# A two-layer hybrid trunk on one core: x and the per-channel parameters handed over by channel, layer 0's sums of squares by a matmul with ones

## The chip, the cores and the metric

One core of a Trainium2 chip runs the whole program. The metric is the device time of one execution in microseconds, as a median over runs. The kernel before took 1278.25 us (median of 3 runs, 1276.6 to 1279.12).

## The reference

Two layers run over 256 tokens of 2048 channels. Cut to what the change touches, each layer is:

```
h    = x * rsqrt(mean(x*x over channels) + eps) * pre_norm_w     # pre-norm, one factor per token
proj = h @ w_in                                                  # 2048 -> 9248 columns: u, gate, z, x, B, C, dt
A    = pool_mixer(u, pool_mix_w, pool_scale) * silu(gate)        # scale per channel
B    = ssd(silu(conv(x,B,C; conv_w, conv_b)), dt; dt_bias, a_log, d_skip), gated by z, times ssd_norm_w
x    = x + rms_norm(concat(A, B) @ w_out, post_norm_w)
```

## The kernel before, in words

**Layout.** Activations stand by channel: a tile `hs` holds, for each of 16 groups of 128 channels (k = 0 to 15), 256 tokens in two parts, a rounded high part and the rest (the low part), 512 columns in all. Weights are split in the same way. They stream in as units of 512 input rows by 512 output columns (`raw`, 1 MB, three buffers). Each unit is split in two halves, a and b, by ScalarE (`wh`, L141) and VectorE (`wl`, L142), five buffers each. A chunk is one 512-column block of the output: four units, u0 to u3 for the first chunk, u4 to u7 for the second. For each 128 by 128 block, TensorE does a wide matmul (high weights by 512 columns, L351) and a narrow one (low weights by the 256 high columns, L353). Here that is called a pair. A chunk has 64 pairs.

**The start of layer 0.** x comes by token in four pieces of 512 channels, into `t` tiles. TensorE turns them by 128 by 128 transposes against an identity (L305). ScalarE makes the high part from the turned block in PSUM, times the pre-norm weight (L314), and VectorE makes the low part (L315). `first_unit` writes out the order of u0 by hand, in single k: its wide and narrow matmuls are L620 and L626, its weight splits L156 and L162 (512 columns wide). Matmuls on the identity (L253) fill TensorE ahead of it. The pre-norm weight is loaded as 32 rows and turned too (L261, L263).

**Sums of squares.** ScalarE squares the untransposed pieces and sums along the row (L322), which gives one number per token. `token_rstd` and `rstd_diag` turn it into a diagonal matrix, and `rstd_spread` multiplies ones by it (L342), so that every partition has the row of factors, copied to `rb` (L344). The factor is applied late, on the output of the projection (L399 on GpSimd). The second chunk (column block C) starts with the 64-column dt block, eight matmuls L725 twice. `dt_chain` multiplies the dt block by `rb` (L422), and two transposes on TensorE follow (L431).

**Parameters.** `load_params` loads four tables as rows and three as broadcast rows. After twelve background steps it turns them by two transposes (L283, L284) and copies them (L285, L289, L290).

**Order.** A list scheduler sets the order of each engine by priorities; each engine then runs its queue strictly in that order. `behind(ins)` puts an instruction after another one of the same engine. Transfers go out from SP and from ScalarE (ACT) and use eight semaphores in turn, so a transfer is issued when the one eight places earlier has landed.

Of the kernel before, what the change touches and what calls it, by code (L numbers as in the profile page):

```python
# [8 lines left out]
F32 = mybir.dt.float32  # L9
# [32 lines left out]
def hybrid_kernel(ctx: ExitStack, tc, x, pre_norm_w, w_in, pool_mix_w, pool_scale, conv_w, conv_b,  # L42
                  dt_bias, a_log, d_skip, ssd_norm_w, w_out, post_norm_w, out):
# [73 lines left out]
    def emit_raw():  # L117
        i = stream["raw"]
        r = wts.tile([P, 4, CW], F32, name="raw", tag="raw", bufs=NRAW)
        src = units[i].rearrange("(k p) c -> p k c", p=P)  # L120
        if i < 2:
            for a, b in (((0, 1), (1, 2), (2, 3), (3, 4)), ((0, 2), (2, 4)))[i]:
                stream["dma"] = nc.sync.dma_start(out=r[:, a:b], in_=src[:, a:b])
        else:
            stream["dma"] = nc.sync.dma_start(out=r, in_=src)
        raws[i] = r
        stream["raw"] += 1
# [66 lines left out]
    def load_pieces(src, between=None):  # L194
        xp.clear()
        for c in range(4):
# [3 lines left out]
            if between is not None and c == 0:  # L200
                for a, b in ((0, 2), (2, 4)):
                    nc.scalar.dma_start(out=v[:, :, a * P:b * P], in_=piece_src[:, :, a * P:b * P])
            else:
                nc.sync.dma_start(out=v, in_=piece_src)
            xp.append(v)
            if between is not None and c < 3:
                between()
# [10 lines left out]
    ones = const.tile([P, P], F32, name="ones")  # L218
    nc.vector.memset(ones, 1.0)
# [29 lines left out]
    pre_cols = const.tile([P, DEPTH * NK], F32, name="pre_cols")  # L249
    def keep_busy(dst, n, after=None):  # L250
        with behind(after):
            for _ in range(n):
                ins = nc.tensor.matmul(dst[:, 0:P], ident, ident, start=True, stop=True, skip_group_check=True)  # L253
        return ins

    with tc.high_priority():
        idle = aux()
        filler = keep_busy(idle, 3)
        pp = aux()
        with behind(filler):  # L260
            pre_t = nc.tensor.transpose(out=pp[:, 0:DEPTH * NK], in_=pre_rows,  # L261
                                        identity=ident[0:DEPTH * NK, 0:DEPTH * NK])
        pre_copy = nc.vector.tensor_copy(pre_cols, pp[:, 0:DEPTH * NK])  # L263
        filler = keep_busy(idle, 4, pre_t)
# [3 lines left out]
    def load_params(l):  # L268
        rows = work.tile([56, P], F32, name="rows", tag="rows", bufs=1)
        nc.sync.dma_start(out=rows[0:16], in_=pool_scale[l].rearrange("(a p) -> a p", p=P))  # L270
        nc.sync.dma_start(out=rows[16:32], in_=ssd_norm_w[l].rearrange("(a p) -> a p", p=P))
        nc.sync.dma_start(out=rows[32:56], in_=conv_b[l].rearrange("(a p) -> a p", p=P))
        rows2 = work.tile([96, P], F32, name="rows2", tag="rows2", bufs=1)
        nc.sync.dma_start(out=rows2, in_=conv_w[l].rearrange("k (a p) -> (k a) p", p=P))
        hb = const.tile([P, 3, NH], F32, name=f"hb{l}")
        nc.sync.dma_start(out=hb[:, 0], in_=dt_bias[l].partition_broadcast(P))
        nc.sync.dma_start(out=hb[:, 1], in_=a_log[l].partition_broadcast(P))
        nc.sync.dma_start(out=hb[:, 2], in_=d_skip[l].partition_broadcast(P))
        for _ in range(12):
            yield  # L280
        cols = const.tile([P, 152], F32, name=f"cols{l}")
        pa = aux()
        nc.tensor.transpose(out=pa[:, 0:56], in_=rows, identity=ident[0:56, 0:56])  # L283
        nc.tensor.transpose(out=pa[:, 56:152], in_=rows2, identity=ident[0:96, 0:96])  # L284
        turned = nc.vector.tensor_copy(cols, pa[:, 0:152])  # L285
        dcol = const.tile([P, 16], F32, name=f"dcol{l}")
        dv = hb[:, 2].rearrange("p (j two) -> p two j", two=2)
        with behind(turned):
            nc.vector.tensor_copy(dcol[0:HD], dv[0:HD, 0])  # L289
            nc.vector.tensor_copy(dcol[HD:P], dv[HD:P, 1])  # L290
        prm[l] = {
            "scale": cols[:, 0:16], "norm": cols[:, 16:32], "convb": cols[:, 32:56],
            "convw": cols[:, 56:152].rearrange("p (k a) -> p k a", k=KCONV), "d": dcol,
            "dtb": hb[:, 0], "alog": hb[:, 1],
# [309 lines left out]
    def piece(c):  # L604
        pts = [None, None]
        transpose_piece(c, range(NT), pts)
        return split_piece(0, c, hs, pts)

    def first_unit(acc):

        pts = [None, None]

        def turn(ks, after):
            with behind(after):
                return transpose_piece(0, range(NT), pts, ks)

        def wide(kk, ms):
            wh = halves[kk // 2][0]
            for m in ms:
# [283 lines left out]
```

## Time and profile before

| | us |
|---|---|
| median of 3 runs | 1278.25 (1276.6 to 1279.12) |
| the profiled execution | 1279.39, its span 1277.7 |
| TensorE (PE) busy | 1265.1, 99% of the span |
| VectorE (DVE) busy | 916.4, 72% |
| ScalarE (ACT) busy | 707.8, 55% |
| GpSimd (POOL) busy | 198.5, 16% |
| DMA | 249.47 MB, mean 195 GB/s |

The span runs from the first to the last instruction; the time of an execution is 1.7 us longer. PE's matmuls overlap each other, so intervals between starts are read as the cost of one, not durations. Times in the rows below count from the start of the span.

### The profile page before, as it was taken

What the parts mean: (1) busy time and instruction counts of PE and PEld (TensorE: products, weight loads), DVE (VectorE), ACT (ScalarE), POOL (GpSimd) and SP (SyncE); (2) the same over time, 40 slices, a digit from 0 to 9 for tenths busy, and PEclk for the clock granted to TensorE, in tenths of its full rate; (3) what the DMA queues carried; (4) which work ended last, traced back from release to release, by engine and by line L of the source; (5) the groups of instructions that cost most, each with busy time, mean ns of one, the idle gap of its engine ahead of it and who ended that gap; (6) DMA issues with size and microseconds to landing.
All of it is one profiled execution on the core that took longest, in us unless ns stands there. A gap on an engine that the chain in (4) does not pass through costs nothing.

```text
span 1277.7 us, 17883 instructions
## 1 busy us (share of the span) xinstructions
PE 1265.1 (99%) x6978; PEld 1087.5 (85%) x6978; DVE 916.4 (72%) x1298; ACT 707.8 (55%) x894; POOL 198.5 (16%) x244
## 2 busy tenths in 40 slices
PE   9999999999999999999999999999999999999997
PEld 8888888888888888888878888888888888888886
DVE  5898778868778794444478978778788788844454
ACT  6656556566466574344374566566565565644442
POOL 0121312212213220000002122122113122200000
PEclk9999999999999999999999999999999999999999
DMA  8555455464474576555564645555654654855652
GB/s 277 200 199 199 165 200 205 152 235 166 164 246 150 212 269 209 189 188 189 188 212 164 220 168 175 204 192 169 226 198 144 219 201 162 296 198 197 197 188 77
DMA packets 127004, 249.47 MB, mean 195 GB/s; under 512 B 9304, under 2 KB 10152, under 8 KB 125640
## 3 DMA queue, kind: packets, MB, share of 16 engines
q1 hardware_dynamic: 124872, 237.27, 54.7%
q0 software_dynamic: 1504, 10.55, 2.2%
q8 instruction: 54, 0.88, 0.3%
q10 hardware_dynamic: 544, 0.52, 0.1%
q14 instruction: 30, 0.25, 0.1%
HBM read 244.06 MB, written 4.26 MB: 194 GB/s over the span
## 4 chain that ended last, share of the span: by engine, by line
PE 98%; ACT 1%; DVE 1%; issue 0%; DMA 0%
PE acc L351 43%; PE acc L353 22%; PE acc L788 9%; PE acc L790 9%; PE acc L789 9%; PE aux L543 1%; PE aux L548 1%; PE aux L725 1%; PE aux L305 1%; PE aux L509 1%; PE acc L620 0%; ACT t L322 0%; PE aux L568 0%; PE aux L497 0%; DVE t L806 0%
## 5 line engine op out<-in xcount | busy, mean ns | idle before, releaser
L351 PE MATMUL acc<-hs,wh 128*128 128x512 f32 x2288 | 804.7, 396 | 1.0 <-DVE hs L315 1.0
L142 DVE TENSOR_TENSOR wl<-raw,wh 128x1024 fp32r<-128x1024 f32 x430 | 531.9, 1246 | 251.8 <-ACT wh L141 251.3
L141 ACT ACTIVATE wh<-raw 128x1024 fp32r<-128x1024 f32 x430 | 450.4, 1058 | 411.3 <-PE acc L351 217.9
L353 PE MATMUL acc<-hs,wl 128*128 128x256 f32 x2288 | 638.7, 279 | 0.0
L351 PEld LDWEIGHTS acc<-hs,wh 128*128 128x128 f32 x2288 | 429.2, 188 | 98.9 <-DVE hs L315 1.5
L353 PEld LDWEIGHTS acc<-hs,wl 128*128 128x128 f32 x2288 | 431.5, 189 | 1.2 <-DVE wl L142 0.2
L399 POOL TENSOR_TENSOR t<-t,rb 128x256 f32<-128x256 f32 x144 | 142.1, 995 | 397.7 <-DVE t L393 369.0
L392 ACT COPY t<-acc 128x256 f32<-128x256 f32 x176 | 62.9, 366 | 70.2 <-PE acc L353 70.1
L788 PE MATMUL acc<-wh,pm 128*128 128x512 f32 x256 | 99.7, 390 | 0.0
L788 PE MATMUL acc<-wh,ms 128*128 128x512 f32 x256 | 99.7, 389 | 0.0
L790 PE MATMUL acc<-wh,ms 128*128 128x512 f32 x256 | 99.7, 389 | 0.0
L790 PE MATMUL acc<-wh,pm 128*128 128x512 f32 x256 | 99.7, 389 | 0.0
L789 PE MATMUL acc<-wl,ms 128*128 128x512 f32 x256 | 99.7, 389 | 0.0
L789 PE MATMUL acc<-wl,pm 128*128 128x512 f32 x256 | 99.6, 389 | 0.0
L393 DVE TENSOR_TENSOR t<-acc,t 128x256 f32<-128x256 f32 x176 | 71.4, 416 | 16.2 <-ACT t L392 15.3
L412 DVE SCALAR_TENSOR_TENSOR t<-t,cols,t 128x256 f32<-128x256 f32 x144 | 72.0, 529 | 0.1
L790 PEld LDWEIGHTS acc<-wh,ms 128*128 128x128 f32 x256 | 48.1, 188 | 10.1
L790 PEld LDWEIGHTS acc<-wh,pm 128*128 128x128 f32 x256 | 48.1, 188 | 10.0
L788 PEld LDWEIGHTS acc<-wh,ms 128*128 128x128 f32 x256 | 48.1, 188 | 10.0
L789 PEld LDWEIGHTS acc<-wl,pm 128*128 128x128 f32 x256 | 48.1, 188 | 9.9
L788 PEld LDWEIGHTS acc<-wh,pm 128*128 128x128 f32 x256 | 48.1, 188 | 9.9
L789 PEld LDWEIGHTS acc<-wl,ms 128*128 128x128 f32 x256 | 48.1, 188 | 9.8
(157 smaller groups left out, 848.3 us busy)
## 6 DMA issues: line engine op xcount, KB each, us to landing
raw<-in_w_in_dram SPq DMA_DIRECT2D x142, 1024.0 KB, 4.9
raw<-in_w_out_dram SPq DMA_DIRECT2D x64, 1024.0 KB, 5.1
t<-acs POOLq DMA_DIRECT2D x8, 1024.0 KB, 5.1
raw<-in_pool_mix_w_dram SPq DMA_DIRECT2D x8, 1024.0 KB, 5.2
t<-in_x_dram SPq DMA_DIRECT2D x7, 512.0 KB, 9.2
pwb<-in_post_norm_w_dram POOLq DMA_DIRECT2D x2, 1024.0 KB, 6.7
x_mid<-t SPq DMA_DIRECT2D x8, 256.0 KB, 2.7
t<-x_mid SPq DMA_DIRECT2D x4, 512.0 KB, 8.9
```

The source lines that it names most:

```text
L141: hi = nc.scalar.activation(out=wh, in_=r, func=AF.Copy)
L142: lo = nc.vector.tensor_tensor(out=wl, in0=r, in1=wh.bitcast(F32), op=ALU.subtract)
L305: ins = nc.tensor.transpose(out=pts[k4 % 2][:, o + T * P:o + (T + 1) * P], in_=xp[c][:, T, k4 * P:(k4 + 1) * P], identity=ident)
L351: nc.tensor.matmul(acc[m], wh[:, kk, cs], mov[:, k0 + kk, :], start=first and kk == 0, stop=False, skip_group_check=True)
L353: stream["mm"] = nc.tensor.matmul(acc[m][:, 0:SEQ], wl[:, kk, cs], mov[:, k0 + kk, 0:SEQ], start=False, stop=last and kk == 1, skip_group_ ...
L392: nc.scalar.copy(out=t[0:n], in_=acc[0:n, SEQ:CW])
L393: nc.vector.tensor_tensor(out=t[0:n], in0=acc[0:n, 0:SEQ], in1=t[0:n], op=ALU.add)
L399: nc.gpsimd.tensor_tensor(out=dest[:, m], in0=t, in1=rb, op=ALU.mult)
L412: nc.vector.scalar_tensor_tensor(out=dst[:, m], in0=pad[:, m, j:j + SEQ], scalar=cw[:, j, ct:ct + 1], in1=dst[:, m], op0=ALU.mult, op1=ALU ...
L788: nc.tensor.matmul(oacc[T], ah, wh[:, kk], start=first and kk == 0, stop=False)
L789: nc.tensor.matmul(oacc[T], ah, wl[:, kk], start=False, stop=False)
L790: nc.tensor.matmul(oacc[T], al, wh[:, kk], start=False, stop=last and kk == 1)
```

## The change

x is also handed over by channel (`x_by_channel`, 128 x 16 x 256: partition, k, token), the pre-norm weight as 128 x 32, and all other parameters of a layer as one table of 128 x 232, built by the host. In layer 0 x goes straight from the transfer into a tile `xt`, and L314 and L315 (now L291 and L292) read it there. Sums of squares are made over channels: four squares of 128 x 1024 (L303), three additions of that size and two smaller ones (L306, L308, L309), one matmul of ones by the total (L314), then square root (L316) and reciprocal (L317) on 128 x 256. The filler becomes eight matmuls on ones, and `load_params` is one transfer. Layer 1 keeps its transposes of x. x by token is still loaded for the residual.

```diff
-    pre_rows = const.tile([DEPTH * NK, P], F32, name="pre_rows")
-    nc.sync.dma_start(out=pre_rows, in_=pre_norm_w.rearrange("l (a p) -> (l a) p", p=P))
-    load_pieces(x_in, emit_raw)
+    nc.sync.dma_start(out=pre_cols, in_=pre_norm_by_channel)
+    xt = t16().rearrange("p a t c -> p (a t c)").rearrange("p (k s) -> p k s", s=SEQ)
+    def load_xt(a, b, queue=nc.sync):
+        queue.dma_start(out=xt[:, a:b], in_=x_by_channel[:, a:b])
+    load_xt(0, 1, nc.scalar)
+    load_xt(1, 2, nc.scalar)
+    emit_raw(lambda: load_xt(2, 4))
+    load_xt(4, 8)
+    emit_raw()
+    load_xt(8, 12)
+    load_xt(12, NK)
+    emit_raw()
...
+        for _ in range(8):
+            filler = nc.tensor.matmul(idle[:, 0:P], ones, ones, start=True, stop=True, skip_group_check=True)
...
-            src = pts[k4 % 2][:, (k4 // 2) * SEQ:(k4 // 2 + 1) * SEQ]
+            src = xt[:, k] if l == 0 else pts[k4 % 2][:, (k4 // 2) * SEQ:(k4 // 2 + 1) * SEQ]
...
+    def square_channels(c, total):
+        sq = t4()[:, :, 0:SEQ]
+        nc.scalar.activation(out=sq, in_=xt[:, 4 * c:4 * c + 4], func=AF.Square)
+        if c == 0:
+            return sq
+        nc.vector.tensor_tensor(out=total, in0=total, in1=sq, op=ALU.add)
+        if c == 3:
+            nc.vector.tensor_tensor(out=total[:, 0:2], in0=total[:, 0:2], in1=total[:, 2:4], op=ALU.add)
+            nc.vector.tensor_tensor(out=total[:, 0], in0=total[:, 0], in1=total[:, 1], op=ALU.add)
+        return total
+    def rstd_channels(total):
+        pb = aux()
+        nc.tensor.matmul(pb[:, 0:SEQ], ones, total[:, 0], start=True, stop=True)
+        rb = work.tile([P, SEQ], F32, name="rb", tag="rb", bufs=1)
+        nc.scalar.activation(out=rb, in_=pb[:, 0:SEQ], func=AF.Sqrt, scale=1.0 / D_MODEL, bias=eps)
+        nc.vector.reciprocal(out=rb, in_=rb)
+        return rb
...
+        hi, lo = filler, None
+        for kk in range(4):
+            with behind(hi, lo):
+                xs = split_piece(0, 0, hs, None, range(kk, kk + 1))
+            hi = first_hi(kk, xs[0])
+            lo = first_lo(kk, xs[1])
+            wide(kk)
+            if kk < 2:
+                narrow(kk)
...
-                    later["rb"] = rstd_spread(later["rd"])
+                    later["rb"] = rstd_spread(later["rd"]) if l else rstd_channels(later["sq"])
```

**PE at the start of the program.** `ident`, `ones` and `pre_rows` are inputs of fillers and transposes, `t_78` is the first piece of x, `hs`, `wh`, `wl` are the split activations and weights. Before:

```order
L253 MATMUL aux<-ident 128x128 x3
L261 MATMUL aux<-ident,pre_rows 128x32
L253 MATMUL aux<-ident 128x128 x4
L305 MATMUL aux<-ident,t_78 128x128 x2
L253 MATMUL aux<-ident 128x128
L620 MATMUL acc<-hs,wh 128x512 x2
L305 MATMUL aux<-ident,t_78 128x128 x2
```

and in the changed kernel:

```order
L261 MATMUL aux<-ones 128x128 x8
L609 MATMUL acc<-hs,wh 128x512 x4
L615 MATMUL acc<-hs,wl 128x256 x4
L609 MATMUL acc<-hs,wh 128x512 x4
L615 MATMUL acc<-hs,wl 128x256 x4
L609 MATMUL acc<-hs,wh 128x512 x8
L615 MATMUL acc<-hs,wl 128x256 x8
```

All 32 transposes of x are gone from the first chunk, and u0 runs in one piece.

**DVE in the first chunk, after u0.** `L315`/`L292` are the low parts of the activations, four k each; `L142`/`L145` are weight halves, in the order u1a, u1b, u2a and so on. Before:

```order
L142 TENSOR_TENSOR wl<-raw,wh 128x1024
L315 SCALAR_TENSOR_TENSOR hs<-aux,pre_cols,hs 128x256 x4
L142 TENSOR_TENSOR wl<-raw,wh 128x1024 x2
L315 SCALAR_TENSOR_TENSOR hs<-aux,pre_cols,hs 128x256 x4
L142 TENSOR_TENSOR wl<-raw,wh 128x1024 x2
L315 SCALAR_TENSOR_TENSOR hs<-aux,pre_cols,hs 128x256 x4
```

and in the changed kernel, where `t_222` is the running total and `t_283`, `t_336`, `t_359` are squares:

```order
L292 SCALAR_TENSOR_TENSOR hs<-s_78,pre_cols,hs 128x256 x4
L145 TENSOR_TENSOR wl<-raw,wh 128x1024 x2
L292 SCALAR_TENSOR_TENSOR hs<-s_78,pre_cols,hs 128x256 x4
L306 TENSOR_TENSOR t_222<-t_222,t_283 128x4x256
L292 SCALAR_TENSOR_TENSOR hs<-s_78,pre_cols,hs 128x256 x4
L306 TENSOR_TENSOR t_222<-t_222,t_336 128x4x256
L145 TENSOR_TENSOR wl<-raw,wh 128x1024 x2
L306 TENSOR_TENSOR t_222<-t_222,t_359 128x4x256
L145 TENSOR_TENSOR wl<-raw,wh 128x1024 x2
```

The first half of u2 stood ahead of the last eight low parts; now it stands behind all of them and behind two additions.

**DVE in the second chunk, up to the product of dt.** `L409`, `L412` (now `L405`, `L408`) are the convolution of block B, `L422` (now `L418`) is the product that the two transposes on PE wait for. Before:

```order
L409 TENSOR_SCALAR t_455<-t_527,cols_447 128x256 x2
L412 SCALAR_TENSOR_TENSOR t_455<-t_527,cols_447,t_455 128x256 x3
L142 TENSOR_TENSOR wl<-raw,wh 128x1024
L412 SCALAR_TENSOR_TENSOR t_455<-t_527,cols_447,t_455 128x256 x2
...
L412 SCALAR_TENSOR_TENSOR t_455<-t_527,cols_447,t_455 128x256 x6
L142 TENSOR_TENSOR wl<-raw,wh 128x1024 x2
L422 TENSOR_TENSOR t_616<-t_616,rb 64x256
```

and in the changed kernel:

```order
L317 RECIPROCAL rb<-rb 128x256
L405 TENSOR_SCALAR t_382<-t_455,cols_149 128x256 x2
L145 TENSOR_TENSOR wl<-raw,wh 128x1024
L408 SCALAR_TENSOR_TENSOR t_382<-t_455,cols_149,t_382 128x256 x2
...
L408 SCALAR_TENSOR_TENSOR t_382<-t_455,cols_149,t_382 128x256 x6
L145 TENSOR_TENSOR wl<-raw,wh 128x1024 x3
L418 TENSOR_TENSOR t_544<-t_544,rb 64x256
```

A reciprocal stands ahead of the convolution, and four weight halves instead of three stand between its start and the product of dt. On PE the two transposes that wait for it stand behind 85 and 86 matmuls of the chunk before, and behind 87 now. Behind this chunk the order on every engine is the same but for the parameter transposes and copies of layer 1.

## Rows read from the trace of the kernel before

**Rows 1.** The page: busy time of engines, and the chain that ended last, by engine.

```profile
PE 1265.1 (99%) x6978; PEld 1087.5 (85%) x6978; DVE 916.4 (72%) x1298; ACT 707.8 (55%) x894; POOL 198.5 (16%) x244
...
PE 98%; ACT 1%; DVE 1%; issue 0%; DMA 0%
```

**Rows 2.** Timeline of the start: start, duration, instruction, idle time before it.

```profile
5.48 0.63 ACT L156 ACTIVATE wh<-raw 128x512 fp32r<-128x512 f32 x1 [2.18 <-DMA raw<-in_w_in_dram]
...
7.40 1.22 PE L620 MATMUL acc<-hs,wh 128*128 128x512 f32 x2 [0.65 <-DVE hs L315]
```

**Rows 3.** Timeline of PE in the first chunk and at its end.

```profile
9.70 1.05 PE L626 MATMUL acc<-hs,wl 128*128 128x256 f32 x4
...
13.10 0.64 PE L626 MATMUL acc<-hs,wl 128*128 128x256 f32 x4
...
17.27 0.39 PE L351 MATMUL acc<-hs,wh 128*128 128x512 f32 x1
...
19.97 0.28 PE L353 MATMUL acc<-hs,wl 128*128 128x256 f32 x1
20.09 1.04 PE L305 MATMUL aux<-ident,t 128*128 128x128 f32 x8
20.88 0.47 PE L351 MATMUL acc<-hs,wh 128*128 128x512 f32 x1
...
35.80 0.28 PE L353 MATMUL acc<-hs,wl 128*128 128x256 f32 x1
...
36.61 2.02 PE L725 MATMUL aux<-hs,wdt 128*64 128x512 f32 x8
```

**Rows 4.** SP's queue: a wait (total, times, longest) and the issue behind it.

```profile
SPq L272 <- DMA t<-in_x_dram: 0.3, 1, 0.3
...
9.48 0.34 SPq L272 DMA_DIRECT2D rows<-in_conv_b_dram  x1
```

**Rows 5.** Groups by line and shape, whole execution: busy us, mean ns | idle before.

```profile
L315 DVE SCALAR_TENSOR_TENSOR hs<-aux,pre_cols,hs 128x256 fp32r<-128x256 f32 x32 | 14.1, 477 | 8.7 <-ACT hs L314 8.2
...
L571 DVE RECIPROCAL t<-t 128x256 f32<-128x256 f32 x8 | 14.0, 1748 | 0.8 <-ACT t L570 0.8
...
L314 ACT ACTIVATE hs<-aux,pre_cols 128x256 fp32r<-128x256 f32 x32 | 13.7, 471 | 11.5 <-PE aux L305 9.7 <-DVE hs L315 1.8
...
L562 ACT ACTIVATE t<-t 128x1024 f32<-128x1024 f32 x8 | 8.5, 1062 | 3.2 <-DVE t L560 3.2
```

**Rows 6.** Transfers issued in the first 40 us: KB each, median us to landing.

```profile
hb<-in_dt_bias_dram SPq DMA_DIRECT2D x2, 16.0 KB, 5.3
...
pre_rows<-in_pre_norm_w_dram SPq DMA_DIRECT2D x1, 16.0 KB, 2.7
```

**Rows 7.** Windows: the second chunk up to dt's transposes, busy us of each engine.

```profile
36.61:55.71 19.10, 19.10 (x104) 15.48 (x104) 19.05 (x35) 11.99 (x17) 3.08 (x4) 1.00 0.50 170
```

**Rows 8.** Timeline of the second chunk on ACT, POOL, DVE and PE.

```profile
41.95 0.37 ACT L344 COPY rb<-aux 128x256 f32<-128x256 f32 x1 [1.34 <-PE aux L342]
...
42.41 3.08 POOL L399 TENSOR_TENSOR t<-t,rb 128x256 f32<-128x256 f32 x4 [16.95 <-ACT rb L344]
...
44.10 1.54 DVE L409 TENSOR_SCALAR t<-t,cols 128x256 f32<-128x256 f32 x2
45.57 1.26 DVE L412 SCALAR_TENSOR_TENSOR t<-t,cols,t 128x256 f32<-128x256 f32 x3
...
52.44 2.34 DVE L142 TENSOR_TENSOR wl<-raw,wh 128x1024 fp32r<-128x1024 f32 x2
54.71 0.41 DVE L422 TENSOR_TENSOR t<-t,rb 64x256 f32<-64x256 f32 x1
...
55.71 0.27 PE L431 MATMUL aux<-ident,t 64*128 64x64 f32 x1
```

**Rows 9.** Timeline of PE at the parameter transposes of layer 1.

```profile
312.74 0.28 PE L353 MATMUL acc<-hs,wl 128*128 128x256 f32 x1
...
313.23 0.48 PE L351 MATMUL acc<-hs,wh 128*128 128x512 f32 x1
```

More of the change, by code (lines that the diff above doesn't have):

```diff
@@ L115, in hybrid_kernel, with emit_raw @@
     halves = {}
-    def emit_raw():
+    def emit_raw(between=None):
         i = stream["raw"]
@@ L123, in emit_raw @@
                 stream["dma"] = nc.sync.dma_start(out=r[:, a:b], in_=src[:, a:b])
+                if between is not None and a == 1:
+                    between()
         else:
@@ L199, in load_pieces @@
             piece_src = src[:, c * CW:(c + 1) * CW].rearrange("(t p) c -> p t c", p=P)
[L200 to L204, printed above, removed]
+            nc.sync.dma_start(out=v, in_=piece_src)
             xp.append(v)
-            if between is not None and c < 3:
-                between()
     x_in = x.rearrange("b s d -> (b s) d")
@@ L275, in load_params @@
[L275 to L290, printed above, removed]
+        cols = const.tile([P, 232], F32, name=f"cols{l}")
+        nc.sync.dma_start(out=cols, in_=per_channel[l])
@@ L604, in piece, with wide @@
     def piece(c):
-        pts = [None, None]
-        transpose_piece(c, range(NT), pts)
-        return split_piece(0, c, hs, pts)
+        return split_piece(0, c, hs, None)
     def first_unit(acc):
[L611 to L617, printed above, removed]
+        def wide(kk):
             wh = halves[kk // 2][0]
-            for m in ms:
+            for m in range(4):
                 stream["mm"] = nc.tensor.matmul(acc[m], wh[:, kk % 2, m * P:(m + 1) * P], hs[:, kk, :],
@@ L627, in narrow @@
                                                 start=False, stop=False, skip_group_check=True)
[L629 to L654 removed]
+        hi, lo = filler, None
[7 more added lines that the diff above has]
+                narrow(kk)
         raws.pop(0)
[L656 removed]
         stream["use"] = 2
[L658 removed]
+        with behind(hi, lo):
             run_ahead(1)
[L660 to L662 removed]
+        return xs, lambda: (narrow(2), narrow(3))
+    with behind(stream["dma"]):
+        load_params(0)
     for l in range(DEPTH):
@@ L685, in first_mid @@
                     later["wd"] = load_wdt(l)
-            if i == 1 and q < 3:
+            if l == 0 and (i == 1 and q < 3 or (q, i) == (3, 0)):
+                with behind(*gate[min(q + 1, 3)]):
+                    later["sq"] = square_channels(q, later.get("sq"))
+            if l and i == 1 and q < 3:
                 with behind(*gate[min(q + 1 + l, 3)]):
@@ L890 @@
     arrays, args = {}, []
+    by_channel = lambda a: a.reshape(-1, 128).T
+    rows = [[inputs[n][l] for n in ("pool_scale", "ssd_norm_w", "conv_b", "conv_w")] for l in range(DEPTH)]
+    heads = [_np.repeat(inputs["d_skip"][l].reshape(-1, 2).T, HD, axis=0) for l in range(DEPTH)]
+    wide = [[_np.tile(inputs[n][l], (128, 1)) for n in ("dt_bias", "a_log")] for l in range(DEPTH)]
+    inputs = dict(inputs,
+                  x_by_channel=inputs["x"].reshape(SEQ, NK, P).transpose(2, 1, 0),
+                  pre_norm_by_channel=by_channel(inputs["pre_norm_w"]),
+                  per_channel=_np.stack([_np.concatenate([by_channel(r) for r in rows[l]] + [heads[l]] + wide[l], axis=1)
+                                         for l in range(DEPTH)]))
     for name in _INS:
```

71 lines of the change are left out of this document (13 added, 58 removed).

## The prediction

> **What bounds the kernel now.** First the page: PE is busy for 1265.1 of 1277.7 us, and the chain that ended last is 98% PE [rows 1]. So DVE, ACT and transfers cost time only where PE waits for them, and the change can gain or lose in three ways: work taken off PE, PE starting earlier, PE waiting in new places. It touches the first 60 us and two transposes in layer 1.
>
> Then the start. PE's first real matmul begins at 7.40, after waiting for the activations; the first weights landed just before 5.48, when ACT began to split them [rows 2]. Four narrow matmuls take 1.05 us at 9.70 and 0.64 at 13.10 [rows 3]: until about 13 PE runs at the lower of its two levels (1.2 GHz), afterwards at 2.4, though the view of windows prints 1.00 throughout. From 17.27 on nothing waits: eight pairs take 17.27 to 20.09, 0.352 each, and eight transposes cost 20.88 - 20.09 = 0.79 [rows 3]. The chunk ends at 35.80 + 0.12 = 35.92, and the dt block follows at 36.61; the 0.69 between them are the two parameter transposes.
>
> In the second chunk the reader should look at DVE, not PE: it is busy for 19.05 of 19.10 us [rows 7], and dt's product ends at 54.71 + 0.41 = 55.12, only 0.6 before the transposes that need it [rows 8]. DVE has no room there.
>
> **Term A, the first chunk.** Removed: 32 transposes, 3.2 us at 0.79 per eight, the waits of the hand-written start, and the 0.69. Taken alone, PE would need 64 x 0.352 = 22.5 us at the higher level.
>
> PE's start. Ahead of the first weights lie now 2 x 128 KB of x instead of 2 x 256 KB. 2.1 MB had landed by 9.48 (below), 0.22 MB per us, so the weights land about 1 us earlier, near 4.5. Their split takes 0.63 [rows 2]; the activations are ready by then. First matmul at 5.2 instead of 7.40. The eight fillers before it replace eight others, are over by then even at 0.5 each, and hide nothing that counts.
>
> But PE does not then run freely. The order of DVE and ACT fixes when the weights of u2 are split: behind all activations and behind two additions. I follow that queue. x for k = 4 to 7 lands at 9.4: in front of it in the queues stand the same 2.1 MB as in front of the second piece of x before, which released SP's next issue at 9.48 [rows 4]. Prices: activation 0.47 on ACT and 0.48 on DVE, 0.42 from one to the next; a 128x1024 square 1.06; a weight half or an addition of that size on DVE 2.34 for two, so 1.12 to 1.2 from one to the next [rows 5, 8]. Additions do not stand in the trace; the weight halves have their shape, and I take 1.14. ACT: hs4 to hs7 until 11.0, u1a 12.0, square 13.0, u1b 14.0. DVE: four low parts until 11.6, waits for u1a, splits it 12.1 to 13.2, waits for u1b, 14.1 to 15.2; then without a gap four low parts (16.9), addition (18.05), four low parts (19.75), addition (20.9), u2a at **22.1**. PE has all wide matmuls of u2a's first four behind it by then, and needs 8 narrow and 4 wide (1.9), u2b (2.8) and u3 (5.6): the chunk ends at 22.1 + 10.3 = **32.4**. Each later step on DVE is ahead of PE: u2b 23.2, u3a 25.5, u3b 26.7, total of squares 29.7, dt's weights 30.4.
>
> This end hardly depends on the clock. If the higher level comes at 9 or 10, PE reaches u2a near 19 and waits about 2 us in two pieces; if it comes at 13, it does not wait. Only after 13 is each us at the lower level paid, at half a us. PE's start is worth 2.2 us and is lost in the same way: the queue on DVE decides. Term A is 32.4 - 36.61 = **-4.2**. Bounds: if PE never waited, 5.2 + 2.4 (4.8 us at the lower level until 10) + 22.5 = 30.1, so -6.5; if x lands 2 us later, every step of the queue moves by 2, so -2.2.
>
> The squares are in ACT's sum above. The matmul of ones by the total has the shape of the old one and the same place: nothing, as its input is done well before.
>
> **Term B, layer 1.** From the narrow matmul at 312.74 to the next wide one at 313.23 are 0.49 us, where 0.12 is normal [rows 9]. Both transposes go: **-0.4**. The copies on DVE behind them cover nothing for PE.
>
> **Term C, the second chunk.** I count from its start (36.61 before). Before, `rb` was there at 41.95 + 0.37 = 42.32, or 5.7; GpSimd multiplied by it from 42.41 for 3.08; DVE's convolution began at 44.10 (7.5) and dt's product ended at 18.5; PE's transposes stood at 55.71 (19.1) [rows 8]. Now ACT takes a square root of 128x256 at 5.34 (0.47 by the nearest row, a table ahead of it is loaded in ACT's idle time), then DVE's reciprocal of 128x256 takes 1.75, where one of 128x2 stood [rows 5]. `rb` is there at 7.65. DVE waits for GpSimd's first product until 8.5, since nothing else stands between. The two L405 and the first weight half run beside GpSimd, and rows show what that costs: two L409 took 1.54 there [rows 8]. They end at 10.0 and 11.5. The rest took 55.12 - 45.57 = 9.55 with three weight halves; one of these has been counted, and there are three more where two stood, so 9.55 again: dt's product ends at 21.1. PE stands at its transposes after 16 dt matmuls (3.85 by eight in 2.02 with the tail [rows 3]), the matmul of ones (0.25, two narrow ones) and 43.5 pairs (15.3), at 19.4. It waits 1.7: **+1.7**. Queued behind them is the rest of the chunk on PE, so the wait is lost whole. Bounds: nothing, if DVE catches up by the 2 us that it was ahead at the chunk's start (it can't by its order: the reciprocal waits for `rb`), and 2.6 if every step beside GpSimd doubles.
>
> What is late next: DVE's steps of `dt_chain` shift with PE, and the next matmul on them stands 121 matmuls (21 us) further on, as before, so I expect no second wait.
>
> **Sum.** -4.2 - 0.4 + 1.7 = -2.9. The profiled execution has span 1277.7 and time 1279.39, so 1276.5 by its own time; it lies 1.1 above the median of 1278.25, which gives **1275.4**.
>
> **A rule against the change.** The pre-norm weight now comes in 128 runs of 128 bytes. Rows: 16 KB in 512-byte rows landed after 2.7 us; the 16 KB broadcast loads, in 128-byte packets but under load, after 5.3 [rows 6]. By the first row ACT starts at 3.6, by the second at 6.1; then it comes to hs4 at 10.0 instead of 9.4, and the sum is 1276.0. The Trainium skill, "DMA: Bandwidth & Descriptors", Specifications, asks for at least 512 B per transfer for line rate and says that below this a read-modify-write is done. I take the first row, since nothing is ahead of it in the queue.
>
> **The rivals.**
> - *No wait at dt's transposes* (1273.7). Speaks for it: DVE enters the chunk further ahead. Against: DVE's order, and 0.6 us of slack before. 0.12.
> - *The first chunk gains only half* (1277.4): x lands 2 us later, or activations from SBUF are slower on DVE. For it: everything hangs on one landing. Against: the same bytes landed by 9.48. With it goes the case that the change does nothing at all (1278.2), if PE waits for DVE in u3 too. Together 0.24.
> - *Slower*: PE's clock. PE now has waits of 0.6, 1.3 and 1.7 us in its first 52 us. If it stayed at, or fell back to, 1.2 GHz through them, each us there costs half (0.64 against 1.05 for the same matmuls, the tail of the last counted in both). 12 us more at the lower level give 1275.4 + 6 = 1281.4; from 11 on the kernel is slower by over 0.2%. Against: before, it rose after a wait of 0.65 at 7.40 [rows 2, 3], and narrow matmuls of 0.28 at 19.97 and 312.74 are both at the higher level [rows 3, 9]. 0.05. The Trainium skill, "TensorE: Matmul & The Clock Gate", Part 1, says that the default state is throttled and activity releases it; the rise at 13 agrees.
>
> The forecast itself has 0.59.
>
> **How the numbers follow.** A measurement of this kernel can tell about 0.2% (2.6 us) from no change. The forecast's own spread is 1274.2 to 1276.8: the wait 1.0 to 2.6, the landing 0.7 either way. It straddles the border of 1275.7, about 0.7 of it on the faster side. Faster: 0.7 x 0.59 + 0.12 = 0.53. Slower 0.05. The rest, 0.42, within 0.2%. The range takes in both middle rivals: 1273.4 to 1277.9.
>
> **What would show it.** Right: L609 begins near 5.2; no transposes of x before layer 1; `wl` of u2a ends near 22, PE waits for it once or twice; the dt block begins at 32.4; PE waits 1 to 2.5 us at L427 for DVE L418, after a reciprocal of 1.75; 0.4 us less at 313. Wrong: a start of the dt block after 34 or before 31; no wait at L427; a granted clock or narrow matmuls of 1.05 us past 15.

## The result, and the profile after

The changed kernel takes **1285.93 us** (median of 6 runs, 1285.19 to 1287.3), the kernel before 1278.11 (6 runs, 1276.6 to 1279.12) beside it: ratio 1.0065, 95% interval 1.0054 to 1.0076, so 7.8 us slower. The profiled execution took 1286.41, its span is 1284.7, which is 7.0 more than before.

The page of the changed kernel, busy time and the chain that ended last, as in [rows 1]:

```profile
PE 1268.4 (99%) x6941; PEld 1086.3 (85%) x6941; DVE 922.9 (72%) x1293; ACT 706.9 (55%) x881; POOL 193.0 (15%) x244
...
PE 95%; DVE 2%; ACT 1%; DMA 1%; issue 0%; SPq 0%; POOL 0%; DVEq 0%
```

TensorE has 37 matmuls fewer, and yet it is busy 3.3 us longer. That is the first hint: a wait adds no busy time (a lower clock would, and is tested below). The timeline of the changed kernel (start, duration, instruction, idle time before it), as in [rows 2, 3, 8], and then on through the run:

```profile
5.64 0.63 ACT L159 ACTIVATE wh<-raw 128x512 fp32r<-128x512 f32 x1 [1.92 <-DMA raw<-in_w_in_dram]
...
6.33 1.24 PE L609 MATMUL acc<-hs,wh 128*128 128x512 f32 x4 [1.81 <-ACT wh L159]
...
9.93 1.03 PE L615 MATMUL acc<-hs,wl 128*128 128x256 f32 x4
...
20.99 1.21 PE L347 MATMUL acc<-hs,wh 128*128 128x512 f32 x4 [1.65 <-ACT wh L144]
...
21.52 2.35 DVE L145 TENSOR_TENSOR wl<-raw,wh 128x1024 fp32r<-128x1024 f32 x2
...
22.78 0.39 PE L349 MATMUL acc<-hs,wl 128*128 128x256 f32 x1 [0.58 <-DVE wl L145]
33.26 1.08 PE L701 MATMUL aux<-hs,wdt 128*64 128x512 f32 x4
...
38.54 0.47 ACT L316 ACTIVATE rb<-aux,eps 128x256 f32<-128x256 f32 x1 [2.32 <-PE aux L314]
39.04 1.75 DVE L317 RECIPROCAL rb<-rb 128x256 f32<-128x256 f32 x1 [2.36 <-ACT rb L316]
...
53.96 0.41 DVE L418 TENSOR_TENSOR t<-t,rb 64x256 f32<-64x256 f32 x1
...
54.52 0.31 PE L427 MATMUL aux<-ident,t 64*128 64x64 f32 x2 [1.79 <-DVE t L418]
...
55.45 0.63 PE L347 MATMUL acc<-hs,wh 128*128 128x512 f32 x1
...
58.62 0.40 PE L347 MATMUL acc<-hs,wh 128*128 128x512 f32 x1
...
100.91 0.38 PE L493 MATMUL aux<-t 128*128 128x256 f32 x1
...
149.71 0.40 PE L347 MATMUL acc<-hs,wh 128*128 128x512 f32 x1
...
152.89 0.40 PE L347 MATMUL acc<-hs,wh 128*128 128x512 f32 x1
...
639.90 0.60 PE L282 MATMUL aux<-ident,t 128*128 128x128 f32 x4
...
1038.88 0.59 PE L493 MATMUL aux<-t 128*128 128x256 f32 x2
```

The same places in the kernel before, so far as [rows 2, 3, 8] do not have them:

```profile
101.31 0.38 PE L497 MATMUL aux<-t 128*128 128x256 f32 x1
...
149.65 0.39 PE L351 MATMUL acc<-hs,wh 128*128 128x512 f32 x1
...
152.77 0.39 PE L351 MATMUL acc<-hs,wh 128*128 128x512 f32 x1
...
636.31 0.49 PE L305 MATMUL aux<-ident,t 128*128 128x128 f32 x3
...
1031.68 0.59 PE L497 MATMUL aux<-t 128*128 128x256 f32 x2
```

Read place by place, after less before: the dt block -3.35 (33.26, 36.61), the dt transposes -1.19 (54.52, 55.71), the first matmul of the first state-space group -0.40, the first transpose of layer 1 **+3.59**, the last state-space group **+7.20**. So the start gains, though less than forecast, and 7.6 us are lost between 101 and 1039, where the order of instructions on TensorE is the same but for two transposes less, and where the view of waits has nothing new for it.

Where they go is seen in the pair rows: nine pairs take 152.89 - 149.71 = 3.18 us after and 152.77 - 149.65 = 3.12 before. Windows of the wide matmul alone (window, length, busy and count on PE, on PEld, granted clock, DMA share, GB/s), changed kernel:

```profile
145.00:190.00 45.00, 45.00 (x129) 23.98 (x128) 1.00 0.60 211
245.00:290.00 45.00, 45.00 (x128) 23.96 (x128) 1.00 0.61 211
```

and before:

```profile
145.00:190.00 45.00, 45.00 (x131) 24.32 (x130) 1.00 0.61 211
245.00:290.00 45.00, 45.00 (x131) 24.39 (x130) 1.00 0.61 211
```

Both run at the granted clock 1.00 and never idle; 131 wide matmuls fit into 45 us before, 128 or 129 after. I took the mean distance from one wide matmul to the next in each stretch between two groups of small matmuls, from all starts in the trace. It has only two values, **346.7 and 353.3 ns** (a stretch has one or the other throughout, but for the last of a layer, which can change within; the short stretches of 47 pairs read about 1 ns more for their first pair). A layer has four groups of chunks with the same small matmuls in each: L509/L505 are transposes against `ident`, L543, L548/L539, L544 read `t` tiles and `scs`, L568/L564 read a `t` tile and `ones`. Stretches and their small matmuls: behind L509/L505 (47 pairs), behind L543, L548/L539, L544 (47 pairs), behind L568/L564 (166 pairs; 62 in the last group of a layer).

| ns a pair, groups 0 to 3 of layer 0, then of layer 1 | before | after |
|---|---|---|
| behind L509 / L505 | 347.5 to 348.7 in all | 347.7 in all |
| behind L548 / L544 | 347.6, 354.2, 354.2, 347.6; 347.6, 354.2, 347.6, 354.2 | 354.3 or 354.4 in all |
| behind L568 / L564 | 346.7 six times; 348.4 and 349.7 in the last groups | 353.4 in all |

That is 6 x 166 x 6.7 ns = 6.7 us, 62 x (5.0 + 3.7) ns = 0.5, and 4 x 47 x 6.7 ns = 1.3: 8.5 us. The two transposes less give back 0.4, and the stretch behind the dt transposes of layer 1, 60 pairs at 347.6 here and at 354.3 before, another 0.4: 7.7, where the places above show 7.6.

The rest of the profile answers to [rows 5 to 7]. Groups by shape of the changed kernel, and its windows (all engines in the order PE, PEld, DVE, ACT, POOL):

```profile
L291 ACT ACTIVATE hs<-s,pre_cols 128x256 fp32r<-128x256 f32 x16 | 7.1, 498 | 1.2 <-DMA s<-in_x_by_channel_dram 1.2
...
L306 DVE TENSOR_TENSOR t<-t,t 128x1024 f32<-128x1024 f32 x3 | 3.6, 1216 | 0.0
```

```profile
5.00:10.00 5.00, 3.67 (x13) 3.09 (x14) 3.69 (x7) 3.50 (x7) 0.00 (x0) 0.74 1.03 370
10.00:15.00 5.00, 5.00 (x29) 4.44 (x28) 2.98 (x6) 4.66 (x8) 0.00 (x0) 0.92 1.04 409
...
33.26:54.52 21.26, 19.46 (x108) 15.88 (x106) 17.45 (x27) 11.20 (x13) 2.94 (x4) 1.00 0.44 153
55.16:58.58 3.42, 3.42 (x12) 2.86 (x12) 1.66 (x5) 1.12 (x2) 0.00 (x0) 0.50 0.93 319
```

The changed kernel's transfer of the pre-norm weight, as in [rows 6]:

```profile
pre_cols<-pre_norm_by_channel_dram SPq DMA_DIRECT2D x1, 16.0 KB, 2.2
```

The pre-norm weight landed 2.2 us after its issue, in its 128-byte runs. After the wait of 1.79 at L427 the granted clock is 0.50, 1.2 GHz, for 3.42 us: five pairs from 55.45 to 58.62 take 3.17 instead of 5 x 0.353.

### The profile page after: what moved, and what is told of

Its sections match the earlier page's. It is cut to its first block, busy times and chain, and to the rows that moved or that the text cites. A ratio compares the mean times of both kernels' runs of the same rounds, so it can differ in the third digit from the quotient of the medians.

```text
span 1284.7 us, 17789 instructions
## 1 busy us (share of the span) xinstructions
PE 1268.4 (99%) x6941; PEld 1086.3 (85%) x6941; DVE 922.9 (72%) x1293; ACT 706.9 (55%) x881; POOL 193.0 (15%) x244
## 4 chain that ended last, share of the span: by engine, by line
PE 95%; DVE 2%; ACT 1%; DMA 1%; issue 0%; SPq 0%; POOL 0%; DVEq 0%
PE acc L347 42%; PE acc L349 22%; PE acc L765 9%; PE acc L764 9%; PE acc L766 9%; PE aux L539 1%; PE aux L544 1%; DVE wl L145 1%; PE aux L505 1%; DMA s<-in_x_by_channel_dram 1%; PE aux L701 0%; ACT wh L144 0%; DVE t L408 0%; ACT t L299 0%; ACT hs L291 0%
## 5 line engine op out<-in xcount | busy, mean ns | idle before, releaser
L347 PE MATMUL acc<-hs,wh 128*128 128x512 f32 x2288 | 813.3, 400 | 2.6 <-ACT wh L144 1.7
L145 DVE TENSOR_TENSOR wl<-raw,wh 128x1024 fp32r<-128x1024 f32 x430 | 535.3, 1253 | 252.5 <-ACT wh L144 252.2
L408 DVE SCALAR_TENSOR_TENSOR t<-t,cols,t 128x256 f32<-128x256 f32 x144 | 71.5, 526 | 0.1
```

Of the source, the lines that this page charges most:

```text
L145: lo = nc.vector.tensor_tensor(out=wl, in0=r, in1=wh.bitcast(F32), op=ALU.subtract)
L347: nc.tensor.matmul(acc[m], wh[:, kk, cs], mov[:, k0 + kk, :], start=first and kk == 0, stop=False, skip_group_check=True)
L408: nc.vector.scalar_tensor_tensor(out=dst[:, m], in0=pad[:, m, j:j + SEQ], scalar=cw[:, j, ct:ct + 1], in1=dst[:, m], op0=ALU.mult, op1=ALU ...
```

## The experiments

The question is what decides which of the two intervals a stretch takes. The theories: PLACE (how many instructions stand ahead on TensorE), ADDRESS (where hs and the weights lie in SBUF), ENTRY (the times at which TensorE reaches each group), CLOCK (falls and rises of the granted clock), SEMAPHORE (the number that TensorE counts up), OPERANDS (where the tiles of the small matmuls lie). Runs without a stated median are single executions; the kernel before took 1276.6 to 1277.4 beside them.

**e1 and e2: one more small product at the start.**

```diff
-        for _ in range(8):                               # after -> e1
+        for _ in range(9):
-        filler = keep_busy(idle, 4, pre_t)               # before -> e2
+        filler = keep_busy(idle, 5, pre_t)
```

> The changed kernel with nine small products at its start in place of eight, nothing else; TensorE's whole stream moves by one instruction. In the trace of the changed kernel a pair (one wide and one narrow matmul) comes every 353.4 ns behind every L539/L544 and L564 group, in the kernel before every 346.7 ns behind L568 and every 346.7 or 353.3 behind L543/L548. Theory PLACE (which interval holds is set by how many TensorE instructions stand ahead): some of these stretches change their interval, the time falls to anywhere in 1278 to 1285. Theory ADDRESS (it is set by where hs, wh and wl lie in SBUF): all stretches keep theirs, 1286 +-0.7. Theory ENTRY (it is set by the state in which the TensorE stream enters each group, that is by timing further up): could go either way, since one filler moves the first wait by about 0.1 us at most.

> The kernel before with five fillers in its second group in place of four, nothing else. PLACE: some of the long stretches behind L568 go from 346.7 to 353.3 ns a pair, and the time rises by 1.1 us for each such stretch, up to about 1286. ADDRESS: stays at 1278.1 +-0.7 with the intervals of before. ENTRY: either.

Measured 1287.05 and 1277.12. Every stretch of the table keeps its interval in both (within 0.3 ns), so one instruction more ahead does not decide, and PLACE falls.

**e3 and e4: hs and the weights moved.**

```diff
+    pad = const.tile([P, 192], F32, name="pad")          # after -> e3
+    hs = big.tile([P, NK, CW], F32R, name="hs", tag="hs", bufs=1)    # ahead of xt, no longer below
+    ms = big.tile([P, NK, CW], F32R, name="ms", tag="ms", bufs=1)
+    pad = const.tile([P, 64], F32, name="pad")           # before -> e4
```

> The changed kernel with hs, ms, the 16-KB-a-partition tile, raw, wh, wl and t8 at the SBUF addresses that they have in the kernel before (768 bytes of padding, and hs and ms allocated ahead of the tile of x); the order of instructions is that of the changed kernel. ADDRESS: the pairs behind L564 come every 346.7 ns again, 8 x 166 pairs x 6.7 ns = about 7 us given back for L564 and part of L539, 1278 to 1280. PLACE and ENTRY: nothing changes, 1286 +-0.7.

> The kernel before with 256 bytes of padding ahead of all its tiles, which gives hs and the weights the offset within 1 KB that they have in the changed kernel; the order of instructions is untouched. ADDRESS (if the offset within a KB is what counts): 353.3 ns a pair behind L568, up to 1286. PLACE and ENTRY: 1278.1 +-0.7 with the intervals of before.

Measured 1286.49 and 1276.47; the wide matmul in e3, in the same window:

```profile
145.00:190.00 45.00, 45.00 (x128) 23.94 (x128) 1.00 0.62 211
```

No stretch of the table changed but the very last of e4 (346.8 for 349.7), so ADDRESS falls for hs and the weights.

**e5 and e6: the wait at L427, and the start.**

```diff
-        nc.vector.tensor_tensor(out=t[0:2 * NH], ..., in1=rb[0:2 * NH], op=ALU.mult)
+        with tc.high_priority(offset=P_EVAC): nc.vector.tensor_tensor(...)      # e5, e6
-        for _ in range(8):
+        for _ in range(16):                                                     # e6
```

> The changed kernel with the dt product (L418) under the high priority of the sums, so that it stands ahead of three weight splits on VectorE and TensorE need not wait 1.79 us at L427; TensorE's order changes by one matmul, the results not at all. All theories: the wait goes, and with it the fall of the granted clock at 55.16 us (3.4 us at the lower level, about 1.7 us): 3.5 us. Theory CLOCK (which of the two pair intervals the long stretches take is set when the granted clock last rose): with no fall at 55 us the stretches behind L539 and L564 change, at best to 346.7 ns as in the kernel before, and the time is 1275.5 +-1. Theory ENTRY (set by the times at which TensorE reaches each group, whatever the clock did): either the stretches stay at 353.4 ns, 1283 +-1, or they change without a rule. Neither: 1283 +-1.

> As the run with the early product, and sixteen small products at the start in place of eight, so that TensorE is not idle for 1.8 us ahead of its first real matmul and the clock has no reason to fall at 7.4 us. CLOCK: the clock rises once and stays; the intervals are set by that one rise and may differ from those of the run with eight fillers; 1274 to 1277 if they are those of the kernel before. ENTRY: no rule; without a change of the intervals 1282 +-1.

Measured 1284.27 and 1283.64. The wait is gone, and the clock no longer falls at 55 us: from the dt transposes to L464 TensorE needs 21.98 instead of 23.17. All stretches of the table stay as they were. The gain was smaller than expected, since in both runs the clock now fell at 22 us. So CLOCK was left in a weaker form: any one fall.

**e7, e8 and e12: a wait put into the kernel before.** Two, one or six reciprocals behind the dt product of layer 0.

```diff
         nc.vector.tensor_tensor(out=t[0:2 * NH], ..., in1=rb[0:2 * NH], op=ALU.mult)
-        yield
+        yield ([nc.vector.reciprocal(out=t[0:2 * NH], in_=t[0:2 * NH]) for _ in range(2)] if l == 0 else None)
```

> The kernel before with two reciprocals put in behind the dt product of layer 0 (x to 1/(1/x), values as before but for rounding), 2 x 1.75 us on VectorE, so that TensorE waits 2 to 3 us at L431; the scheduler shifts some of what follows. CLOCK: the granted clock falls at about 57 us, and some of the long stretches behind L543 and L568 take 353.4 ns: 1277 + 2.9 + 1.7 + up to 7 = 1282 to 1289. ENTRY: 1281 to 1282, or without a rule.

> The control of it: one reciprocal (the dt product of layer 0 comes out as its inverse, a changed result), 1.75 us on VectorE, a wait of about 1.1 us at L431, too short to drop the clock if the one of 1.79 us was near the least that does. CLOCK: no fall, intervals behind L568 stay 346.7 ns, 1278 +-1. ENTRY: the intervals change as in the run with two reciprocals.

> The kernel before with six reciprocals behind the dt product of layer 0 (an even number, so the values come back but for rounding), so that TensorE waits for several us at L431 and the clock falls near 56 us and rises again. CLOCK: from there on pairs behind L568 at 353.4 ns, about 1290. SEMAPHORE and ENTRY: they stay at 346.7, the wait and some 2 us for the clock alone, 1282 to 1287.

Measured 1279.47, 1277.89 and 1280.54. The scheduler moved the transposes behind the longer chain, so TensorE waited 1.3, 1.4 and 0.6 us only at L431 and the clock never fell: for CLOCK they tell nothing. For ENTRY they do. All three reach the groups at other times, e12 even has one stretch behind L509 at 354.2, and yet all others but the last of a layer take the pattern of before. But for that one stretch ENTRY falls.

**e9: no fall of the clock in the changed kernel.**

```diff
+            [nc.tensor.matmul(idle[:, 0:P], ones, ones, start=True, stop=True, ...)     # on top of e6
+             for _ in range({(0, 1): 2, (1, 1): 9}.get((q, i), 0) if l == 0 else 0)]
```

> The changed kernel with the early product, sixteen small products at its start, and two and nine more in the two places of the first chunk where TensorE waited for weights (L347 at about 12 and 20 us), so that the clock has no wait of over 1 us to fall in. All runs of the changed kernel so far had at least one fall of the granted clock and all runs of the kernel before none, so a weaker form of CLOCK still stands: one fall and rise, wherever it is, decides which pair intervals the whole run takes. CLOCK: with one rise and no fall the long stretches behind L564 come at 346.7 ns, 1275 +-1.5. Theory SEMAPHORE or anything else that lies in the program and not in time (TensorE's stream counts up semaphore 103 in the changed kernel and 110 in the kernel before): they stay at 353.4 ns, 1282.5 +-1.

Measured 1282.37. The clock rose at 4.1 us and stayed; the wide matmul:

```profile
145.00:190.00 45.00, 45.00 (x128) 23.87 (x128) 1.00 0.60 200
```

CLOCK falls altogether. (In e10 below the clock rose once, at 9.3 us, and did not fall either.)

**e10 and e11: small products on the other tile.** `ones` and `ident` exchanged in the fillers of each kernel.

```diff
-            filler = nc.tensor.matmul(idle[:, 0:P], ones, ones, ...)      # after -> e10
+            filler = nc.tensor.matmul(idle[:, 0:P], ident, ident, ...)
-                ins = nc.tensor.matmul(dst[:, 0:P], ident, ident, ...)    # before -> e11
+                ins = nc.tensor.matmul(dst[:, 0:P], ones, ones, ...)
```

> The changed kernel with its eight first products on ident instead of ones: they start when GpSimd has built it, a little later, and the scheduler's order and TensorE's semaphore number (109 in place of 103) change with that. SEMAPHORE: pairs behind L564 at 346.7 ns, 1279 +-1. CLOCK: depends on whether the clock still falls at 7 and 55 us; if it does, 353.4 ns, 1286 +-1.

> The kernel before with its small products on ones instead of ident, as in the changed kernel: TensorE's semaphore number is 103 then. SEMAPHORE: pairs behind L568 at 353.4 ns, about 1284 to 1286. CLOCK: no fall, 346.7 ns, 1277 +-1.

Measured 1283.73 and 1278.87. e11 has TensorE's semaphore at 103 and the pattern of before (131 wide matmuls in 45 us); e10 has it at 109 and the pattern of after. SEMAPHORE falls. From about 60 us on the instructions of all engines, their order and TensorE's waits are the same in both kernels but for the parameter steps; only addresses and PSUM banks were left.

**e13, e14 and e15: tiles moved, no instruction changed.** Read from the built programs: `ones`, `ident` and the two masks begin at 128 modulo 256 bytes before and at 0 after; `t4`, `t1` and `scs` likewise; hs and the weights at 128 in both. Other tiles move with them: `eps`, `table` and `fac` with `ones`; `rb`, `xr` and `e` with `t1`, and `dt`, `adt` and `acs` too, at 0 before and 128 after; in e14 also `t2`; in e15 hs and the weights by 256 bytes, which keeps their 128. So the runs sort by two groups of tiles, not by single operands.

```diff
+    _ = [t4() for _ in range(6)], [sums_tile() for _ in range(2)], [t2() for _ in range(3)], \
+        [work.tile([P, 2], F32, name="s2", tag="s2", bufs=4) for _ in range(4)]     # after -> e13
+    pad = work.tile([P, 32], F32, name="pad")                                       # before -> e14
+    pad = const.tile([P, 32], F32, name="pad"); ones = ...                          # after -> e15
+    prm = {}; pad2 = const.tile([P, 32], F32, name="pad2")
```

> The changed kernel, every instruction and its order untouched, with the small working tiles laid out in the order of the kernel before, so that the tiles that feed the small matmuls (t4, t1, scs) begin at 128 modulo 256 bytes as there; in the changed kernel and in its variants they begin at 0 modulo 256, in the kernel before and its variants at 128. hs and the weights stay where they are. Theory OPERANDS (the offset of the small matmuls' operands decides the state in which the pairs behind them run): pairs behind L564 at 346.7 ns, 1278 to 1280. If it is none of these offsets: 353.4 ns, 1286 +-1.

> The kernel before, every instruction and its order untouched, with 128 bytes of padding ahead of its working tiles: t4, t1 and scs begin at 0 modulo 256 bytes, as in the changed kernel. OPERANDS: pairs behind L568 at 353.4 ns, 1284 to 1285. Otherwise 346.7 ns, 1277 +-1.

> The changed kernel, every instruction and its order untouched, with 128 bytes ahead of ones, ident and the two masks and 128 behind the constants: these four begin at 128 modulo 256 bytes as in the kernel before, all else keeps its offset. If it is the offset of ones (weights of L564) that decides: 346.7 ns behind L564, 1278 to 1280. If it is t4, t1 and scs, or none: 1286 +-1.

Measured 1279.72, 1276.11 and 1278.11. The wide matmul in e13:

```profile
145.00:190.00 45.00, 45.00 (x131) 24.31 (x130) 1.00 0.63 211
```

and in e15:

```profile
145.00:190.00 45.00, 45.00 (x131) 24.32 (x130) 1.00 0.61 209
```

In e15 two pads of 128 bytes give 7.8 us back with every instruction untouched. Of the 8.3 us between the two profiled executions some 7.4 are intervals, and 0.7 were gained ahead of the first group. Moving the working tiles in the kernel before did not give the time of after, as OPERANDS in its simple form had it, but another pattern. Sorted by both offsets, all runs fall into four patterns:

| `ones`, `ident`, masks | `t4`, `t1`, `scs` | behind L505 | behind L544 | behind L564 | seen in |
|---|---|---|---|---|---|
| 128 | 128 | 347.6 | 347.6 and 354.2, about half each | 346.7 | before, e2, e4, e7, e8, e11, e12, e16 to e18 |
| 0 | 0 | 347.7 | 354.3 | **353.4** | after, e1, e3, e5, e6, e9, e10 |
| 0 | 128 | 347.7 | 354.2 | 346.7 | e13 |
| 128 | 0 | 354.2 | 347.7 | 346.7 | e14, e15 (in the first group of a layer 347.7, then 354.2; not so in layer 0 of e14) |

e14 and e15 come from different kernels and share their pattern, but for one group: the offsets decide, not the change.

**e16: one part of the change alone**, parameters by channel in the kernel before (the new `load_params` and its table, nothing else of the diff).

> One part of the change alone, in the kernel before: parameters by channel in both layers (one transfer of 928 bytes a partition in place of eight, no L283/L284 transposes); x is still transposed and its squares summed by token. Its working tiles keep the offsets of the kernel before. OPERANDS: 346.7 ns behind L568, 1275.5 to 1277, the 0.4 us of the layer-1 transposes gained. If the part itself (one group of small matmuls less, all groups evenly spaced) decides: 353.4 ns in some or all of the long stretches, up to 1284.

Measured 1277.58 beside 1277.39: no change that one execution could show, and the pattern of 128 and 128.

**e17 and e18: the change at equal offsets, and a version without its waits.** e17 is e13 and e15 together. e18 adds e6 and this:

```diff
+SQ = {(0, 1): 0, (1, 1): 1, (2, 0): 2, (2, 1): 3}
-            if l == 0 and (i == 1 and q < 3 or (q, i) == (3, 0)):
-                with behind(*gate[min(q + 1, 3)]):
-                    later["sq"] = square_channels(q, later.get("sq"))
+            if l == 0 and (q, i) in SQ:
+                with behind(*(stream["last"] if SQ[q, i] else gate[1])):
+                    later["sq"] = square_channels(SQ[q, i], later.get("sq"))
-                with behind(*gate[3]):
+                with behind(*gate[3]), tc.high_priority(offset=0 if l else 2 * P_EVAC):   # split_wdt
```

> The changed kernel, every instruction and its order untouched, with both groups of tiles (ones, ident and the masks; t4, t1 and scs) at 128 modulo 256 bytes, the pair of offsets of the kernel before. Theory OPERANDS, as it stands after the four runs on offsets: both groups at 0 modulo 256 give 353.4 ns behind L544 and behind L564 (1286); one group at 0 gives it in one of the three stretches of a group of chunks, 1278 to 1280; both at 128 give the pattern of the kernel before, 353.3 behind every second L544 alone. The time is then 1277.5 +-1, which is the change itself at equal offsets: its first chunk gains 2 to 3 us and gives them back in the wait at L427 and the fall of the clock there. If the pattern is not that of before, offsets modulo 256 are not the whole rule.

> The same offsets, and the waits of the first stages taken out: the dt product early (as in the fifth run), sixteen small products at the start, the squares of x behind the weight splits that TensorE waits for at 20 us (1.7 us), and the split of the dt weights ahead of the sums. Results unchanged. By the sum of the parts: 1277.5 less 1.8 for L427, 1.7 for the clock at 55 us, 1 to 1.7 for the wait at 20 us: 1272.5 to 1273.5, faster than the kernel before by 0.3 to 0.4%. If the gain of the first chunk is given back in yet another wait: 1275 to 1277.

e17: 1277.34 (11 runs, 1275.74 to 1278.97), ratio to before **1.0001** [0.9992, 1.001]. Its profiled execution took 1275.74; the dt block and the wait:

```profile
32.30 1.08 PE L701 MATMUL aux<-hs,wdt 128*64 128x512 f32 x4
...
53.59 0.31 PE L427 MATMUL aux<-ident,t 64*128 64x64 f32 x2 [1.82 <-DVE t L418]
```

Here the clock did not fall after the wait. Of the eleven runs the three with a mean granted clock of 0.996 are the slowest (1278.42 to 1278.97), and the three fastest (1275.74 to 1276.12) have 0.998. So the spread of 3 us goes with the clock, though not all of it: the kernel before spreads from 1276.16 to 1278.46 beside it, at 0.998 and 0.999. With the same instructions as the changed kernel, and only addresses moved, the median falls from 1285.93 to 1277.34, and the ratio to the kernel before from 1.0065 to 1.0001.

e18: **1272.43** (5 runs, 1272.21 to 1272.61), ratio 0.9963 [0.9949, 0.9977], faster than the kernel before (1277.0 beside both, 15 runs) by 4.6 us. The dt block and the transposes, and all waits of TensorE:

```profile
30.48 0.85 PE L701 MATMUL aux<-hs,wdt 128*64 128x512 f32 x3
...
49.53 0.27 PE L427 MATMUL aux<-ident,t 64*128 64x64 f32 x1
```

```profile
PE aux L261 <- DVE eps L236: 1.1, 1, 1.1
PE acc L347 <- DVE hs L292: 1.0, 1, 1.0
PE aux L701 <- DVE wdt L254: 0.9, 1, 0.9
PE acc L349 <- DVE wl L145: 0.3, 1, 0.3
```

With the squares behind the weight splits the wait of 1.65 at u2 is gone, and the dt block comes 6.1 us earlier than in the profile of before. The time lies at the lower edge of the sum forecast for it; the terms of that sum were not measured singly, and against the profiled execution of e17, where the clock did not fall at 55 us, e18's 1272.5 is 3.2 us less.

## Why the prediction was wrong

**The failed step** is the first one: that the change can gain or lose in three ways only, by work taken off PE, by its start, by new waits. There is a fourth, the interval at which the same matmuls follow each other. The prediction took 0.352 for a pair from one place of the first chunk and let the other 1,220 us cost what they cost before, because their order is the same. Stretch by stretch they cost 8.5 us more, since the removed and shortened constants moved every later tile. e13, e15 and e17 show it by address alone, with every instruction as in the changed kernel. No rival in the prediction has this mechanism.

**Term A, -4.2, measured -3.35.** For the changed kernel the mechanism was right: DVE's queue decided. u2a's low part ended near 22.7 (21.52 and half of 2.35) instead of 22.1: the activations of k = 4 began at 10.34, not 9.4, and an addition costs 1.22. The first weights did not land earlier in this execution: their split began at 5.64, before at 5.48 [rows 2], forecast 4.5. That cost the start 1.1 us (6.33 for 5.2) and the end of the chunk little, as the prediction said. With the wait at u2 TensorE paid in two pieces, 1.65 (for ScalarE's half) and 0.58, as foreseen. The missing 0.85 is in part the draw of one execution. The first activation of k = 4 in the changed kernel and in e17, which has the same instructions:

```profile
10.34 0.51 ACT L291 ACTIVATE hs<-s,pre_cols 128x256 fp32r<-128x256 f32 x1 [1.19 <-DMA s<-in_x_by_channel_dram]
```

```profile
9.39 0.51 ACT L291 ACTIVATE hs<-s,pre_cols 128x256 fp32r<-128x256 f32 x1 [0.38 <-DMA s<-in_x_by_channel_dram]
```

There x landed as forecast (9.39 for 9.4), and the dt block began as forecast (32.30 for 32.4). In the eight traces with this first chunk it begins between 32.30 and 34.11, latest in the five where the clock fell at 22 us (e1, e3, e5, e6, e13: 33.6 to 34.1). "This end hardly depends on the clock" held for its rise, not for such a fall.

What the prediction had wrong here is the other side of the difference. It took 36.61 as the place of the dt block before, but that too is one execution, in which the higher clock came as late as 13. In e14, the same instructions as before, the narrow matmuls are at the higher level by 8.25:

```profile
8.25 0.63 PE L626 MATMUL acc<-hs,wl 128*128 128x256 f32 x4
...
33.95 0.42 PE L725 MATMUL aux<-hs,wdt 128*64 128x512 f32 x1
...
53.02 0.27 PE L431 MATMUL aux<-ident,t 64*128 64x64 f32 x1
```

In the nine traces of the kernel before and its variants the dt block comes broadly the later, the later the granted clock rose: at 33.95 with a rise at 6.1 us (e4, e14), at 35.36 with one at 10.75 (e16), at 36.61 with the latest, at 13.06. By the medians of these traces, 35.21 and 33.66, the first chunk gains 1.55 us and not 4.2, and the 1.7 of term C takes them back. That fits the ratio of 1.0001 in e17.

**Term B, -0.4.** It can't be read singly in the changed kernel. In e17 the group of chunks that held the two transposes, from one L509 (L505) to the next, takes 99.31 instead of 100.03 us: the 0.4 and 47 x 6.6 ns = 0.3, for the stretch behind it takes the other interval there.

**Term C, +1.7, measured 1.79.** Step by step as worked out from the chunk's start: the reciprocal ended 7.5 us into it (7.65), dt's product 21.1 (21.1), TensorE stood at its transposes at 19.5 (19.4).

**The sum.** -3.35 + 1.79 = -1.56, where -2.5 was forecast; with 0.37 for a pair more ahead of the transposes this is the -1.19 at them. "I expect no second wait" was right, but the fall of the clock behind the wait was not in the sum: five pairs took 3.17 us there instead of 1.77, 1.4 more. At equal offsets and without that fall the profiled execution of e17 took 1275.74, next to the forecast of 1275.4, but that is luck of the base: the kernel before took 1277.0 beside it, not 1278.25, so 1.3 us were gained and not 2.9. The median of e17, 1277.34, gains nothing.

**The slower rival** named the right place, a fall to 1.2 GHz in the waits, and it came twice, at 7 and 55 us (windows 5:10 and 55.16:58.58), but for 3.4 us each. It is not what made the kernel slower than before: e9, with no fall and no wait at L427, is still at 1282.37, 5.7 above. **The rule against the change** did not bite: the weight landed after 2.2 us, close to the 2.7 of [rows 6] for 512-byte rows.

## What to carry to other kernels

When two programs differ by under 1%, compare the interval of equal work in equal stretches before looking for waits: counts per window show it, mean durations (396 and 400 ns here) hardly do. A change that only removes or shrinks tiles moves all others; measure it at equal offsets too, with padding, before its worth is judged. A wait on the engine that bounds everything can have a second price, when its clock falls behind it (1.4 us behind one of 1.79 here). And the start of one profiled execution is one draw: before a term is taken as a difference from it, see how far the same place moves between executions (2.7 us here).

## What was not expected of the hardware

The offsets in SBUF of two groups of tiles, the operands of the small matmuls among them, decided how fast the 47 or 166 pairs behind a small matmul ran, 346.7 or 353.3 ns, although these pairs read other tiles; but for the last stretch of a layer, one rate holds until the next small matmuls. Four pairs of offsets gave four patterns, which came back in every run but for single first and last stretches; one of the four was seen in one run only, e13. The Trainium skill, "SBUF — State Buffer", Operand start alignment, asks that an operand start at a multiple of its element size and says that its runs timed nothing; all offsets here meet that, and the spread is 8 us in 1,280.

What stays open: why the interval has two values and how a small matmul hands its state on; which tile of each group decides, and whether it is an operand of the small matmuls or a tile that moved with them; whether 256 bytes is the true period (only 0 and 128 were tried); when the clock first rises, between 4.0 and 13.1 us in these traces; and when a wait drops the clock, since 1.79 us at L427 did in one execution and 1.82 in another did not.
